# One of four column blocks of each MLP's second product made by seven half-block products (Strassen)

## The chip, the cores and the metric

The kernel runs on one core of a Trainium2 chip. The metric is the device time of one execution in microseconds (us). Three timed runs of the kernel before took 2242.58, 2242.69 and 2243.5 us; their median is 2242.69 us. The trace shown here is of one further, profiled execution of 2241.86 us, whose first and last instructions are 2240.1 us apart (its span). The engines are TensorE (PE; its weight loads are shown as PEld), VectorE (DVE), ScalarE (ACT), GpSimd (POOL) and SyncE (SP, whose queue issues the loads of weights).

## What is computed

A two-layer transformer over 256 tokens of width 2048 in float32. Layer 0 has stick-breaking attention, layer 1 a sparse attention of three branches; each is followed by an MLP with squared ReLU, 2048 to 8192 to 2048. The part that matters:

```python
def rms_norm(x, g):
    y = xf * lax.rsqrt(jnp.mean(xf * xf, axis=-1, keepdims=True) + NORM_EPS)
    return (y * g).astype(x.dtype)

def sqrelu_mlp(h, w1, w2):
    return jnp.square(jax.nn.relu(h @ w1)) @ w2

for layer in range(2):
    h = h + attention[layer](rms_norm(h, norm_g[layer]), ...)
    h = h + sqrelu_mlp(rms_norm(h, mlp_norm_g[layer]), mlp_w1[layer], mlp_w2[layer])
```

## The kernel before

**Products in three parts.** Every float32 product is made of three products of rounded parts: a matrix is split into `hi`, its value rounded to the matrix engine's float32r form, and `lo`, the rest; `x@w` is made as xhi·whi + xlo·whi + xhi·wlo, all gathered in one PSUM bank. `split` (line 122) makes `hi` on ScalarE (line 124) and `lo` on VectorE (line 126) for each chunk of weights, 128 partitions by 2 times 512 values, 512 KB, which `load` (line 131) brings through SP's queue. There are five buffers for raw chunks, four for `hi` and four for `lo`. A load waits until an older chunk's `lo` is made; a `hi` waits until TensorE has done with an older `hi`.

**The MLP** (`mlp`, line 351) goes through the 8192 hidden values in four groups `fg` of 2048. In a group's first product, four blocks `fb` of 512 hidden values are made transposed by `proj_T2` (line 185): eight chunks a block, each eight matmuls over 512 columns (line 192) and eight over 256 (line 198), into four PSUM banks. Lines 363 to 372 turn each pair of banks into squared ReLU values: ScalarE copies half a bank (`part`, line 367), VectorE adds the other half (`pre`, line 368) and forms max(a, 0)·a (`sq`, line 370), ScalarE rounds it (`yhi`, line 371) and VectorE makes the rest (`ylo`, line 372). The norm's factor is not in y: its square `r2` (line 361), one number per token, is multiplied in where a result is added to `h`.

In the group's second product, y is multiplied with four column blocks `nb` of w2, one after the other. Each is eight calls of `chunk_N` (line 142), a chunk being two rows of 128 hidden values by 512 columns; twelve matmuls over 512 columns (line 146), eight with `hi` and then four with `lo`, into two banks, one per half of the tokens. `add_h` (line 314) adds the two banks, times r2, to `h`.

**PSUM** has eight banks in two pools of four, `acc` and `att`. The blocks `fb` take acc and att in turn; the second product takes acc for nb 0 and 1 and att for nb 2 and 3 (acc for all in a layer's last group).

**The order of the work.** A scheduler lays out each engine's instructions when the program is built; on the chip every engine goes through its own list strictly in that order. Generators that are spawned (`spawn`, `pump`, lines 101 to 114) put pieces of other work between the chunks: `next_x` (line 287) transposes the new h into the next product's input, one block after `done(nb)`. `bcast_rows` (line 307) lays a per-token factor out along a row, by two small TensorE transposes (line 311).

Of the kernel before, what the change touches and what calls it, by code (L numbers as in the profile page):

```python
# [8 lines left out]
F32 = mybir.dt.float32  # L9
F32R = mybir.dt.float32r  # L10
AF = mybir.ActivationFunctionType
OP = mybir.AluOpType
# [3 lines left out]
P = 128  # L16
T = 256
NT = T // P
D = 2048
KD = D // P  # L20
# [19 lines left out]
def hybrid_kernel(  # L40
# [9 lines left out]
    wraw = ctx.enter_context(tc.tile_pool(name="wraw", bufs=5))  # L50
    whi = ctx.enter_context(tc.tile_pool(name="whi", bufs=4))
    wlo = ctx.enter_context(tc.tile_pool(name="wlo", bufs=4))
    acc = ctx.enter_context(tc.tile_pool(name="acc", bufs=4, space=PSUM))
    att = ctx.enter_context(tc.tile_pool(name="att", bufs=4, space=PSUM))

# [45 lines left out]
    def spawn(gen, rate, wait=0.0, first=False):  # L101
        beside.insert(0 if first else len(beside), [gen, rate, -wait])
# [122 lines left out]
    def evac_T2(dst, ps, row):  # L225
# [4 lines left out]
            nc.vector.tensor_tensor(dst[:, j, :], ps[j][:, :T], c[:, j, :], op=OP.add)  # L230
        nc.vector.tensor_tensor(dst, dst, row.unsqueeze(1).to_broadcast([P, 2, T]), op=OP.mult)

    def proj_N(src, n0, pool=acc, tag="acc"):
# [88 lines left out]
    def add_out(nb, ps, scale, ov):  # L322

        for t in range(NT):
            for i in range(2):
                w = NB // 2
                c = slice(nb * NB + i * w, nb * NB + (i + 1) * w)
                nc.vector.scalar_tensor_tensor(
                    h[:, t, c], ps[t][:, i * w:(i + 1) * w], scale[:, t:t + 1], h[:, t, c], op0=OP.mult, op1=OP.add
                )  # L330
                (nc.sync, nc.scalar)[i].dma_start(ov[:, t, c], h[:, t, c])

    def out_proj(src, layer, g0):
# [16 lines left out]

    def mlp(l, layer, junk, done, last=None):
        w1, w2 = mlp_w1[l], mlp_w2[l]
        r2 = None
        for fg in range(DFF // D):
            for fb in range(D // NB):
                ps = [bank(*((acc, "acc"), (att, "att"))[fb % 2]) for _ in range(NB // P)]
                proj_T2(ps, w1, fg * D + fb * NB)
                if r2 is None:
                    rstd = make_rstd(layer)
                    r2 = small.tile([P, NT], F32, tag="r2", name="r2")  # L360
                    nc.vector.tensor_tensor(r2, rstd, rstd, op=OP.mult)
# [11 lines left out]
            for nb in range(D // NB):  # L373
                end = last is not None and fg == DFF // D - 1 and nb == D // NB - 1
                pool = (att, "att") if nb >= 2 and fg < DFF // D - 1 else (acc, "acc")
                ps = [bank(*pool) for _ in range(NT)]
                for k0 in range(0, KD, KC):
                    chunk_N(ps, w2, fg * KD + k0, nb * NB, k0 == 0, k0 + (KC, 2 * KC)[end] == KD, yhi, ylo, koff=fg * KD,
                            by_token=end and k0 + KC == KD)
                if end:  # L380
                    add_out(nb, ps, r2, last)
                    return
                add_h(nb, ps, r2)
                if fg == DFF // D - 1:
                    done(nb)


    with tc.tile_pool(name="sbp", bufs=2) as sp:
# [195 lines left out]
    nc.vector.tensor_copy(peT, ppe[:, :2 * CL])  # L584

    with tc.tile_pool(name="m0p", bufs=2) as mp:
        def done0(nb):
            spawn(next_x("nsa", nb, G_NSA), 1)

        mlp(0, "m0", mp, done0)  # L590

# [350 lines left out]
        out_proj(nsa_w_out[0], "m1", G_M1)  # L942

    with tc.tile_pool(name="m1p", bufs=2) as mp:
        ov = out[0].rearrange("(t p) d -> p t d", p=P)
# [35 lines left out]
```

## Time and profile before

| | |
|---|---|
| median of three runs | 2242.69 us |
| profiled execution | 2241.86 us |
| its span | 2240.1 us |
| TensorE matmuls busy | 2231.1 us, 100% |
| TensorE weight loads busy | 1876.6 us, 84% |
| VectorE busy | 1309.9 us, 58% |
| ScalarE busy | 1099.1 us, 49% |
| granted TensorE clock, mean | 1.00 (2.4 GHz) |
| DMA | 405.86 MB, 181 GB/s |

Busy is the time in which at least one instruction of the engine was under way; neighbouring matmuls overlap, so the mean length of one matmul is longer than the step from one to the next. The chain of waits gives the steps: a piece of it is so many matmuls in so much time. In the same way a line of the timeline gives when an instruction began, and the difference of two beginnings is what one instruction really holds its engine for when the next stands ready.

The trace has the first MLP from 403 to 1123 us and the second from 1518 us to the end; in each, a group's first product takes about 90 us and its second about 89 us.

### The profile page before, as it was taken

What the parts mean: (1) busy time and instruction counts of PE and PEld (TensorE: products, weight loads), DVE (VectorE), ACT (ScalarE), POOL (GpSimd) and SP (SyncE); (2) the same over time, 40 slices, a digit from 0 to 9 for tenths busy, and PEclk for the clock granted to TensorE, in tenths of its full rate; (3) what the DMA queues carried; (4) which work ended last, traced back from release to release, by engine and by line L of the source; (5) the groups of instructions that cost most, each with busy time, mean ns of one, the idle gap of its engine ahead of it and who ended that gap; (6) DMA issues with size and microseconds to landing.
All of it is one profiled execution on the core that took longest, in us unless ns stands there. A gap on an engine that the chain in (4) does not pass through costs nothing.

```text
span 2240.1 us, 29460 instructions
## 1 busy us (share of the span) xinstructions
PE 2231.1 (100%) x11342; PEld 1876.6 (84%) x11342; DVE 1309.9 (58%) x1706; ACT 1099.1 (49%) x1591; POOL 43.1 (2%) x75
## 2 busy tenths in 40 slices
PE   9999999999999999999999999999999999999999
PEld 9888888888888888888887888888888888888887
DVE  5656655564555465556577877755655555654554
ACT  5555665443444344345455666655434434443442
POOL 0000000000000000000000011000000000000000
PEclk9999999999999999999999999999999999999999
DMA  6655555665665665665567554456656656656664
GB/s 228 201 166 170 166 166 181 185 187 188 189 188 188 189 188 188 189 188 188 179 177 218 160 142 142 133 167 184 188 185 192 188 187 190 186 185 193 187 197 136
DMA packets 260758, 405.86 MB, mean 181 GB/s; under 512 B 13189, under 2 KB 91913, under 8 KB 260617
## 3 DMA queue, kind: packets, MB, share of 16 engines
q1 hardware_dynamic: 259800, 403.52, 58.9%
q8 instruction: 89, 1.46, 0.3%
q10 hardware_dynamic: 816, 0.46, 0.1%
q14 instruction: 53, 0.43, 0.1%
HBM read 401.83 MB, written 2.10 MB: 180 GB/s over the span
## 4 chain that ended last, share of the span: by engine, by line
PE 99%; DVE 0%; POOL 0%; ACT 0%; issue 0%; DVEq 0%; ACTq 0%; POOLq 0%
PE acc L146 39%; PE att L146 13%; PE acc L192 11%; PE att L192 11%; PE att L198 5%; PE acc L198 5%; PE acc L212 5%; PE acc L218 3%; PE acc L175 2%; PE att L262 1%; PE att L814 1%; PE att L806 0%; PE att L807 0%; PE att L808 0%; PE att L502 0%; PE att L550 0%
## 5 line engine op out<-in xcount | busy, mean ns | idle before, releaser
L126 DVE TENSOR_TENSOR lo<-raw,hi 128x1024 fp32r<-128x1024 f32 x751 | 918.0, 1224 | 757.7 <-ACT hi L124 747.3
L124 ACT ACTIVATE hi<-raw 128x1024 fp32r<-128x1024 f32 x751 | 795.2, 1060 | 1032.1 <-PE acc L146 374.9
L146 PE MATMUL acc<-hi,yhi 128*128 128x512 f32 x892 | 354.0, 397 | 0.0
L146 PE MATMUL acc<-hi,ylo 128*128 128x512 f32 x892 | 351.6, 394 | 0.0
L192 PE MATMUL acc<-xs,hi 128*128 128x512 f32 x1024 | 259.6, 395 | 0.0
L192 PE MATMUL att<-xs,hi 128*128 128x512 f32 x1024 | 259.1, 395 | 0.0
L146 PE MATMUL acc<-lo,yhi 128*128 128x512 f32 x892 | 244.5, 395 | 0.0
L192 PEld LDWEIGHTS acc<-xs,hi 128*128 128x128 f32 x1024 | 184.0, 188 | 34.7 <-DVE h L318 0.3
L192 PEld LDWEIGHTS att<-xs,hi 128*128 128x128 f32 x1024 | 183.7, 188 | 33.9
L146 PEld LDWEIGHTS acc<-hi,yhi 128*128 128x128 f32 x892 | 168.1, 188 | 38.1 <-ACT yhi L248 0.2
L146 PEld LDWEIGHTS acc<-lo,yhi 128*128 128x128 f32 x892 | 167.4, 188 | 38.8 <-issue 0.4
L146 PEld LDWEIGHTS acc<-hi,ylo 128*128 128x128 f32 x892 | 168.1, 188 | 37.6 <-DVE ylo L249 0.2
L146 PE MATMUL acc<-hi,xs 128*128 128x512 f32 x704 | 180.0, 396 | 0.0
L146 PEld LDWEIGHTS acc<-hi,xs 128*128 128x128 f32 x704 | 130.7, 188 | 28.7
L146 PE MATMUL att<-hi,ylo 128*128 128x512 f32 x384 | 151.6, 395 | 0.0
L146 PE MATMUL att<-hi,yhi 128*128 128x512 f32 x384 | 151.5, 394 | 0.0
L198 PEld LDWEIGHTS att<-xs,lo 128*128 128x128 f32 x1024 | 139.3, 188 | 11.8
L198 PEld LDWEIGHTS acc<-xs,lo 128*128 128x128 f32 x1024 | 139.3, 188 | 11.8
L198 PE MATMUL att<-xs,lo 128*128 128x256 f32 x1024 | 142.2, 281 | 0.0
L198 PE MATMUL acc<-xs,lo 128*128 128x256 f32 x1024 | 142.2, 281 | 0.0
L212 PE MATMUL acc<-xs,hi 128*128 128x512 f32 x512 | 130.5, 396 | 0.0
L212 PEld LDWEIGHTS acc<-xs,hi 128*128 128x128 f32 x512 | 91.9, 188 | 17.5 <-DVE xs L269 0.3
(234 smaller groups left out, 1942.4 us busy)
## 6 DMA issues: line engine op xcount, KB each, us to landing
raw<-in_mlp_w_dram SPq DMA_DIRECT2D x512, 512.0 KB, 3.9
raw<-in_sb_w_qkv_dram SPq DMA_DIRECT2D x95, 512.0 KB, 3.8
raw<-in_nsa_w_in_dram SPq DMA_DIRECT2D x50, 512.0 KB, 3.6
raw<-in_sb_w_out_dram SPq DMA_DIRECT2D x32, 512.0 KB, 3.8
raw<-in_nsa_w_in_dram SPq DMA_DIRECT2D x64, 256.0 KB, 3.2
raw<-in_nsa_w_out_dram SPq DMA_DIRECT2D x32, 512.0 KB, 3.9
w1t<-in_nsa_cmp_w_dram SPq DMA_DIRECT2D x8, 512.0 KB, 4.0
h<-in_x_dram SPq DMA_DIRECT2D x8, 256.0 KB, 4.3
```

The source lines that it names most:

```text
L124: nc.scalar.activation(hi, raw, AF.Copy)
L126: nc.vector.tensor_tensor(lo, raw, hi.bitcast(F32), op=OP.subtract)
L146: mm = lambda a, b, k, t, s, e: nc.tensor.matmul(ps[t], a[:, k, t * P:(t + 1) * P], b, start=s, stop=e)
L175: nc.tensor.matmul(o, w[:, kk, m * P:(m + 1) * P], x[:, k0 + kk, :], start=s, stop=e, skip_group_check=True)
L192: nc.tensor.matmul(ps[m], hi[:, kk, m * P:(m + 1) * P], xs[:, k0 + kk, :, :].rearrange("p a t -> p (a t)"), start=k0 + kk == 0, stop=k0 + ...
L198: nc.tensor.matmul(ps[m][:, :T], lo[:, kk, m * P:(m + 1) * P], xhi[:, k0 + kk, :], start=False, stop=k0 + kk == KD - 1, skip_group_check=True,
L212: nc.tensor.matmul(ps[m], hi[:, kk, m * P:(m + 1) * P], xs[:, k0 + kk, :, :].rearrange("p a t -> p (a t)"), start=k0 + kk == 0, stop=k0 + ...
L218: nc.tensor.matmul(ps[m][:, :T], lo[:, kk, m * P:(m + 1) * P], xhi[:, k0 + kk, :], start=False, stop=k0 + kk == KD - 1, skip_group_check=True,
L262: nc.tensor.transpose(ps[:, j * T + t * P:j * T + (t + 1) * P], h[:, t, (kp + j) * P:(kp + j + 1) * P], ident)
L814: nc.tensor.transpose(ptp[:w, j * P:(j + 1) * P], src(j), ident)
```

## The change

In each group of both MLPs, the column block nb = 2 is no longer made by twelve matmuls over 512 columns a chunk but by Strassen's scheme (Winograd's form) on the 2-by-2 blocks that a chunk and the two halves of the tokens form: seven products, each half a block wide. With three rounded parts each, that is 21 matmuls over 256 columns a chunk (`chunk_S`), into seven half banks. For this:

- sums of y blocks (`sums`, split into the tile `ss`) are made where y is made, 128 columns each, four per pair of banks;
- sums of the weights' blocks (`ts`) are made on VectorE for each chunk of block 2, and then split like a chunk, so that such a chunk takes two of the four `hi` buffers and two of the four `lo` buffers;
- the seven half banks are put together and added to `h` by `add_S`;
- the norm's factor goes into y, as (max(a, 0)·r)², since the sums run over tokens: `row` holds r along the tokens (by `bcast_rows`, once in each MLP), line 370 becomes a multiplication with it, and the square is made on ScalarE. `add_h` and `add_out` lose their factor;
- the order of the second product changes. Chunks of block 2 stand between chunks of blocks 0 and 1, one after every two; block 3 follows alone. In a layer's last group the order begins with two chunks of block 2, and `done` is called for blocks 0 to 2 together when block 3 begins. The two PSUM pools change their roles from group to group, since block 2 now holds four banks.

```diff
+    def chunk_S(ps, src, k0, n0, first, last, ahi, alo, shi, slo, koff=0):
+        W = NB // 2
+        raw = load(src, k0, KC, n0, NB)
+        flat = raw.rearrange("p k n -> p (k n)")
+        ts = wsum.tile([P, 4, W], F32, tag="ts", name="ts")
+        b12 = flat[:, 3 * W:].unsqueeze(1).to_broadcast([P, 2, W])
+        nc.vector.tensor_tensor(ts[:, :2, :], flat[:, W:3 * W].rearrange("p (a n) -> p a n", a=2), b12, op=OP.subtract)
...
+        nc.scalar.activation(hi[:, :3 * W], flat[:, :3 * W], AF.Copy)
+        nc.vector.tensor_tensor(ts[:, 2, :], ts[:, 0, :], flat[:, 2 * W:3 * W], op=OP.add)
+        nc.vector.tensor_tensor(ts[:, 3, :], flat[:, :W], ts[:, 2, :], op=OP.subtract)
+        thi, tlo = split(ts)
+        nc.vector.tensor_tensor(lo[:, :3 * W], flat[:, :3 * W], hi[:, :3 * W].bitcast(F32), op=OP.subtract)
...
+        for i, xh, xl, wh, wl in trivial + sums:
+            mm(i, xh, wh, first and i in (0, 1, 6, 4), False)
+            mm(i, xl, wh, False, False)
+        pump()
+        for i, xh, xl, wh, wl in sums + trivial:
+            mm(i, xh, wl, False, last)
+        pump()
...
+    def add_S(nb, bs, ps, pool):
...
+        nc.scalar.activation(u[:, 0, :], ps[0], AF.Copy)
+        nc.vector.tensor_tensor(v[:, 0, :], ps[5], u[:, 0, :], op=OP.add)
+        nc.vector.tensor_tensor(u[:, 1, :], ps[4], v[:, 0, :], op=OP.add)
+        nc.vector.tensor_tensor(v[:, 1, :], ps[6], v[:, 0, :], op=OP.add)
+        nc.vector.tensor_tensor(hb[0], bs[1], hb[0], op=OP.add)
+        nc.vector.tensor_tensor(hb[1], bs[2], hb[1], op=OP.add)
+        nc.vector.tensor_tensor(hb[0], hb[0], u.rearrange("p a n -> p (a n)"), op=OP.add)
+        hv = hb[1].rearrange("p (a n) -> p a n", a=2)
+        nc.vector.tensor_tensor(hv, hv, v[:, 1, :].unsqueeze(1).to_broadcast([P, 2, W]), op=OP.add)
...
+        def rows():
+            yield
+            pb = bcast_rows(make_rstd(layer))
+            nc.scalar.activation(row, pb[:, :T], AF.Copy)
...
                         nc.vector.tensor_tensor(a[:, j, :], ps[2 * b + j][:, :T], c[:, j, :], op=OP.add)
+                    nc.vector.scalar_tensor_tensor(
+                        a, a, 0.0, row.unsqueeze(1).to_broadcast([P, 2, T]), op0=OP.max, op1=OP.mult
+                    )
                     s = junk.tile([P, 2, T], F32, tag="sq", name="sq")
-                    nc.vector.scalar_tensor_tensor(s, a, 0.0, a, op0=OP.max, op1=OP.mult)
+                    nc.scalar.activation(s, a, AF.Square)
                     nc.scalar.activation(yhi[:, k:k + 2, :], s, AF.Copy)
                     nc.vector.tensor_tensor(ylo[:, k:k + 2, :], s, yhi[:, k:k + 2, :].bitcast(F32), op=OP.subtract)
+                    a1, a2 = [[s[:, kk, t * P:(t + 1) * P] for kk in (1, 0)] for t in range(NT)]
+                    q = junk.tile([P, 4, P], F32, tag="sums", name="sums")
+                    nc.vector.scalar_tensor_tensor(q[:, 0, :], a2[0], -1.0, a2[1], op0=OP.mult, op1=OP.subtract)
+                    nc.vector.tensor_tensor(q[:, 2, :], a1[0], a2[0], op=OP.subtract)
+                    nc.vector.tensor_tensor(q[:, 1, :], a2[1], q[:, 2, :], op=OP.subtract)
+                    nc.vector.tensor_tensor(q[:, 3, :], a1[1], q[:, 1, :], op=OP.subtract)
+                    split_evac(ss[:, 0, k // 2], ss[:, 1, k // 2], q)
...
+            for i in range(NK):
+                pq = [(j // NK, j % NK) for j in (2 * i, 2 * i + 1)]
+                order += [(2, i)] + pq if end else pq + [(2, i)]
+            if end:
+                order.insert(1, order.pop(3))
+            order += [(3, i) for i in range(NK)]
...
+            group1(fg, ((A, B), (B, A))[fg % 2])
+            group2(fg, *((A, B) if end or fg % 2 == 0 else (B, A)), end)
...
-            spawn(next_x("nsa", nb, G_NSA), 1)
+            spawn(next_x("nsa", nb, G_NSA), 1.5)
```

What this makes of the engines' lists is seen at two places. The first is TensorE, at the first chunk of block 2 in the first MLP's first group (line 147 of the new kernel is line 146 of the old one; line 268 is `chunk_S`; `ss` holds the sums of y).

```order
L147 MATMUL acc<-lo,yhi 128x512 x4
L268 MATMUL att<-hi,yhi 128x256
L268 MATMUL att<-hi,ylo 128x256
L268 MATMUL att<-hi,yhi 128x256
L268 MATMUL att<-hi,ylo 128x256
L268 MATMUL att<-hi,ss 128x256 x8
L268 MATMUL att<-hi,yhi 128x256
L268 MATMUL att<-hi,ylo 128x256
L268 MATMUL att<-lo,ss 128x256 x3
L268 MATMUL att<-lo,yhi 128x256 x3
L268 MATMUL att<-lo,ss 128x256
```

Between two plain chunks there now stand 14 matmuls with a `hi` (six with the chunk's own, eight with that of its sums) and 7 with a `lo`, all over 256 columns and into the att pool.

The second is VectorE where the first MLP's last group goes over from its first to its second product. Before, the list there is this (lines 368 to 372 are the last block's way from PSUM to y, line 126 is the `lo` of chunks to come):

```order
L126 TENSOR_TENSOR lo<-raw,hi 128x1024 x6
L368 TENSOR_TENSOR pre<-att,part 128x256 x3
L370 SCALAR_TENSOR_TENSOR sq<-pre 128x512
L368 TENSOR_TENSOR pre<-att,part 128x256
L126 TENSOR_TENSOR lo<-raw,hi 128x1024
L372 TENSOR_TENSOR ylo<-sq,yhi 128x512
L370 SCALAR_TENSOR_TENSOR sq<-pre 128x512
L126 TENSOR_TENSOR lo<-raw,hi 128x1024
```

In the changed kernel the same place reads as follows (line 127 is the old line 126, the first row of it for the sums of the second chunk of block 2; line 250 the `lo` of that chunk itself; lines 439, 440 and 446 the old 368, 370 and 372; lines 450 to 453 the sums of y):

```order
L127 TENSOR_TENSOR lo<-ts,hi 128x1024
L439 TENSOR_TENSOR pre<-acc,part 128x256 x3
L440 SCALAR_TENSOR_TENSOR pre<-pre,row 128x512
L439 TENSOR_TENSOR pre<-acc,part 128x256
L250 TENSOR_TENSOR lo<-raw,hi 128x768
L450 SCALAR_TENSOR_TENSOR sums<-sq 128x128
L446 TENSOR_TENSOR ylo<-sq,yhi 128x512
L451 TENSOR_TENSOR sums<-sq 128x128
L440 SCALAR_TENSOR_TENSOR pre<-pre,row 128x512
L452 TENSOR_TENSOR sums<-sq,sums 128x128
L127 TENSOR_TENSOR lo<-raw,hi 128x1024
```

The last row is the `lo` of the first plain chunk, the third chunk that TensorE takes in this product. Five instructions stand before it that follow on ScalarE's square of the same block.

## Rows read from the trace of the kernel before

**Rows 1.** The page: busy time of each engine with its share of the span, and two of its rows of tenths in 40 slices.

```profile
PE 2231.1 (100%) x11342; PEld 1876.6 (84%) x11342; DVE 1309.9 (58%) x1706; ACT 1099.1 (49%) x1591; POOL 43.1 (2%) x75
...
PE   9999999999999999999999999999999999999999
...
DVE  5656655564555465556577877755655555654554
```

**Rows 2.** The chain of waits in order of time: start in us, length in us, engine, pool and line, number of matmuls. The first pieces are of a stretch of the first product and the turn to the second (first MLP, group 0); the next lie in the first projection, where matmuls over 256 columns alone follow each other.

```profile
485.65 1.86 PE att L192 x8
487.51 0.94 PE att L198 x8
...
494.08 44.61 PE acc L146 x192
...
43.49 5.70 PE acc L175 x48
...
49.62 8.54 PE acc L175 x72
...
1031.47 27.89 PE acc L146 x120
```

**Rows 3.** Groups of the page and of the list by line: line, engine, operation, tiles, shapes, number | busy us, mean ns of one | idle us before. The short matmul and its weight load.

```profile
L198 PEld LDWEIGHTS acc<-xs,lo 128*128 128x128 f32 x1024 | 139.3, 188 | 11.8
...
L198 PE MATMUL acc<-xs,lo 128*128 128x256 f32 x1024 | 142.2, 281 | 0.0
```

**Rows 4.** Busy time by stretch (us): length, then busy time and number of instructions of PE, PEld, DVE, ACT and POOL, the granted clock, the DMA engines' busy share and GB/s. The first stretch is a first product, the second a second product.

```profile
403.00:494.00 91.00, 91.00 (x522) 79.56 (x522) 53.07 (x66) 43.50 (x59) 0.70 (x1) 1.00 0.62 185
494.00:583.00 89.00, 89.00 (x385) 72.18 (x384) 46.80 (x46) 35.97 (x39) 0.00 (x0) 1.00 0.60 189
```

**Rows 5.** Groups of VectorE and then of ScalarE with shapes kept apart, columns as in rows 3.

```profile
L126 DVE TENSOR_TENSOR lo<-raw,hi 128x1024 fp32r<-128x1024 f32 x751 | 918.0, 1224 | 757.7 <-ACT hi L124 747.3 <-PE acc L146 2.8 <-ACT e L510 2.6
L372 DVE TENSOR_TENSOR ylo<-sq,yhi 128x512 fp32r<-128x512 f32 x64 | 43.7, 683 | 0.0
L370 DVE SCALAR_TENSOR_TENSOR sq<-pre 128x512 f32<-128x512 f32 x64 | 43.7, 682 | 0.0
...
L320 DVE SCALAR_TENSOR_TENSOR h<-acc,r,h 128x512 f32<-128x512 f32 x38 | 26.8, 746 | 22.2 <-PE acc L146 22.2
...
L368 DVE TENSOR_TENSOR pre<-acc,part 128x256 f32<-128x256 f32 x64 | 23.9, 415 | 0.0
...
L318 DVE TENSOR_TENSOR h<-acc,h 128x512 f32<-128x512 f32 x16 | 10.3, 686 | 7.7 <-PE acc L146 7.6
...
L615 DVE TENSOR_SCALAR dist<-dg 128x128 f32<-128x128 f32 x2 | 0.5, 278 | 0.0
...
L124 ACT ACTIVATE hi<-raw 128x1024 fp32r<-128x1024 f32 x751 | 795.2, 1060 | 1032.1 <-PE acc L146 374.9 <-PE acc L192 186.9 <-PE att L146 179.3
L371 ACT ACTIVATE yhi<-sq 128x512 fp32r<-128x512 f32 x64 | 40.1, 627 | 2.9 <-DVE sq L370 0.5
...
L367 ACT ACTIVATE part<-acc 128x256 f32<-128x256 f32 x64 | 19.0, 381 | 0.0
```

**Rows 6.** The timeline of VectorE and then of ScalarE where the first MLP's last group turns to its second product (at 1031.47 us, rows 2): start, length in us, engine, line, operation, tiles, shapes, number, and in brackets the idle time before and what ended it.

```profile
1031.66 1.23 DVE L126 TENSOR_TENSOR lo<-raw,hi 128x1024 fp32r<-128x1024 f32 x1 [1.58 <-ACT hi L124]
1032.80 1.08 DVE L368 TENSOR_TENSOR pre<-att,part 128x256 f32<-128x256 f32 x3
1033.80 0.68 DVE L370 SCALAR_TENSOR_TENSOR sq<-pre 128x512 f32<-128x512 f32 x1
1034.40 0.42 DVE L368 TENSOR_TENSOR pre<-att,part 128x256 f32<-128x256 f32 x1
1034.73 1.21 DVE L126 TENSOR_TENSOR lo<-raw,hi 128x1024 fp32r<-128x1024 f32 x1
1035.86 0.68 DVE L372 TENSOR_TENSOR ylo<-sq,yhi 128x512 fp32r<-128x512 f32 x1
1036.47 0.68 DVE L370 SCALAR_TENSOR_TENSOR sq<-pre 128x512 f32<-128x512 f32 x1
1037.29 1.22 DVE L126 TENSOR_TENSOR lo<-raw,hi 128x1024 fp32r<-128x1024 f32 x1
...
1030.57 1.06 ACT L124 ACTIVATE hi<-raw 128x1024 fp32r<-128x1024 f32 x1 [1.75 <-PE att L192]
1031.53 1.18 ACT L367 ACTIVATE part<-att 128x256 f32<-128x256 f32 x4
1033.37 1.06 ACT L124 ACTIVATE hi<-raw 128x1024 fp32r<-128x1024 f32 x1 [0.66 <-PE acc L146]
```

**Rows 7.** The list of waits (who waited for whom: us in total, times, longest us), and of the page the loads of the MLPs' weights (number, KB each, median us from issue to landing).

```profile
DVE lo L126 <- ACT hi L124: 747.3, 553, 2.2
...
ACT hi L124 <- PE acc L146: 374.9, 244, 2.6
...
raw<-in_mlp_w_dram SPq DMA_DIRECT2D x512, 512.0 KB, 3.9
```

**Rows 8.** The chain of waits near the start of layer 1, columns as in rows 2: the two transposes of `bcast_rows`.

```profile
1133.63 0.22 PE att L311 x2
```

More of the change, by code (lines that the diff above doesn't have):

```diff
@@ L231, in evac_T2, with mm @@
         nc.vector.tensor_tensor(dst, dst, row.unsqueeze(1).to_broadcast([P, 2, T]), op=OP.mult)
+    def chunk_S(ps, src, k0, n0, first, last, ahi, alo, shi, slo, koff=0):
[5 more added lines that the diff above has]
+        nc.vector.tensor_tensor(ts[:, :2, :], flat[:, W:3 * W].rearrange("p (a n) -> p a n", a=2), b12, op=OP.subtract)
+        hi = whi.tile([P, KC, NB], F32R, tag="hi", name="hi").rearrange("p k n -> p (k n)")
+        lo = wlo.tile([P, KC, NB], F32R, tag="lo", name="lo").rearrange("p k n -> p (k n)")
+        nc.scalar.activation(hi[:, :3 * W], flat[:, :3 * W], AF.Copy)
[3 more added lines that the diff above has]
+        nc.vector.tensor_tensor(lo[:, :3 * W], flat[:, :3 * W], hi[:, :3 * W].bitcast(F32), op=OP.subtract)
+        k = k0 - koff
+        y = lambda a, kk, t: a[:, k + kk, t * P:(t + 1) * P]
+        s = lambda a, i: a[:, k // KC, i, :]
+        b = lambda w, i: w[:, i * W:(i + 1) * W]
+        trivial = [
+            (0, y(ahi, 1, 0), y(alo, 1, 0), b(hi, 2), b(lo, 2)),
+            (1, y(ahi, 0, 0), y(alo, 0, 0), b(hi, 0), b(lo, 0)),
+            (2, s(shi, 3), s(slo, 3), b(hi, 1), b(lo, 1)),
+        ]
+        sums = [
+            (6, s(shi, 2), s(slo, 2), thi[:, 0, :], tlo[:, 0, :]),
+            (4, s(shi, 0), s(slo, 0), thi[:, 1, :], tlo[:, 1, :]),
+            (5, s(shi, 1), s(slo, 1), thi[:, 2, :], tlo[:, 2, :]),
+            (3, y(ahi, 0, 1), y(alo, 0, 1), thi[:, 3, :], tlo[:, 3, :]),
+        ]
+        def mm(i, a, w, s, e):
+            nc.tensor.matmul(ps[i], a, w, start=s, stop=e, skip_group_check=True)
+        for i, xh, xl, wh, wl in trivial + sums:
[5 more added lines that the diff above has]
+        pump()
@@ new lines, in banks_S @@
+    def banks_S(pool, tag):
+        W = NB // 2
+        bs = [bank(pool, tag) for _ in range(4)]
+        half = lambda j, i: bs[j][:, i * W:(i + 1) * W]
+        return bs, [half(0, 0), half(1, 0), half(1, 1), half(2, 0), half(2, 1), half(3, 1), half(3, 0)]
+    def add_S(nb, bs, ps, pool):
+        W = NB // 2
+        u = pool.tile([P, 2, W], F32, tag="part", name="u")
+        v = pool.tile([P, 2, W], F32, tag="pre", name="v")
+        hb = [h[:, t, nb * NB:(nb + 1) * NB] for t in range(NT)]
+        nc.scalar.activation(u[:, 0, :], ps[0], AF.Copy)
[7 more added lines that the diff above has]
+        nc.vector.tensor_tensor(hv, hv, v[:, 1, :].unsqueeze(1).to_broadcast([P, 2, W]), op=OP.add)
@@ L327, in add_out @@
                 c = slice(nb * NB + i * w, nb * NB + (i + 1) * w)
-                nc.vector.scalar_tensor_tensor(
-                    h[:, t, c], ps[t][:, i * w:(i + 1) * w], scale[:, t:t + 1], h[:, t, c], op0=OP.mult, op1=OP.add
-                )
+                nc.vector.tensor_tensor(h[:, t, c], ps[t][:, i * w:(i + 1) * w], h[:, t, c], op=OP.add)
                 (nc.sync, nc.scalar)[i].dma_start(ov[:, t, c], h[:, t, c])
@@ L352, in mlp, with group1 @@
         w1, w2 = mlp_w1[l], mlp_w2[l]
-        r2 = None
-        for fg in range(DFF // D):
+        ss = junk.tile([P, 2, KD // 2, 4, P], F32R, name="ss", bufs=1)
+        row = junk.tile([P, T], F32, name="row", bufs=1)
+        def rows():
+            yield
+            pb = bcast_rows(make_rstd(layer))
+            nc.scalar.activation(row, pb[:, :T], AF.Copy)
+        def group1(fg, pools):
             for fb in range(D // NB):
-                ps = [bank(*((acc, "acc"), (att, "att"))[fb % 2]) for _ in range(NB // P)]
+                ps = [bank(*pools[fb % 2]) for _ in range(NB // P)]
                 proj_T2(ps, w1, fg * D + fb * NB)
[L358 to L361, printed above, removed]
                 for b in range(2):
@@ L371, in mlp @@
                     nc.scalar.activation(yhi[:, k:k + 2, :], s, AF.Copy)
                     nc.vector.tensor_tensor(ylo[:, k:k + 2, :], s, yhi[:, k:k + 2, :].bitcast(F32), op=OP.subtract)
[L373 to L385, printed above, removed]
+                    a1, a2 = [[s[:, kk, t * P:(t + 1) * P] for kk in (1, 0)] for t in range(NT)]
@@ new lines, in group2 @@
+        def group2(fg, plain, strassen, end):
+            NK = KD // KC
+            order = []
+            for i in range(NK):
[4 more added lines that the diff above has]
+            order += [(3, i) for i in range(NK)]
+            for nb, i in order:
+                k0 = fg * KD + i * KC
+                args = (w2, k0, nb * NB, i == 0, i == NK - 1, yhi, ylo)
+                if nb == 2:
+                    if i == 0:
+                        bs, s = banks_S(*strassen)
+                    chunk_S(s, *args, ss[:, 0], ss[:, 1], koff=fg * KD)
+                    if i == NK - 1:
+                        add_S(nb, bs, s, junk)
+                    continue
+                if i == 0:
+                    ps = [bank(*plain) for _ in range(NT)]
+                    if end and nb == 3:
+                        for n in range(3):
+                            done(n)
+                out = last is not None and end and nb == 3
+                chunk_N(ps, w2, k0, nb * NB, i == 0, i == NK - (2 if out else 1), yhi, ylo, koff=fg * KD,
+                        by_token=out and i == NK - 1)
+                if i == NK - 1:
+                    if out:
+                        add_out(nb, ps, last)
+                        return
+                    add_h(nb, ps)
+                    if end and nb == 3:
+                        done(nb)
@@ L388, in hybrid_kernel @@
+        spawn(rows(), 1)
+        A, B = (acc, "acc"), (att, "att")
+        for fg in range(DFF // D):
+            end = fg == DFF // D - 1
+            group1(fg, ((A, B), (B, A))[fg % 2])
+            group2(fg, *((A, B) if end or fg % 2 == 0 else (B, A)), end)
     with tc.tile_pool(name="sbp", bufs=2) as sp:
@@ L944, in hybrid_kernel @@
     with tc.tile_pool(name="m1p", bufs=2) as mp:
+        wsum = mp
         ov = out[0].rearrange("(t p) d -> p t d", p=P)
```

4 lines of the change are left out of this document (3 added, 1 removed).

## The prediction

> **What bounds the kernel now.** I read the page first. TensorE is busy for 2231.1 us of a span of 2240.1, in every one of 40 slices, while VectorE has 58% and ScalarE 49% [rows 1]. So one asks first how many TensorE steps there are, and only then whether another engine comes late. The chain of waits confirms it: it runs from one TensorE piece to the next without a gap, and it gives the steps [rows 2]. In the second product 192 matmuls over 512 columns take 44.61 us: 232.3 ns each, 2.788 us for a chunk of twelve. Where matmuls over 256 columns alone follow each other, 72 take 8.54 us: 118.6 ns each; the 48 before them give 118.8. Eight between longer ones take 0.94 us, 117.5 ns each. The short step is thus 0.51 of the long one, although a weight load is listed with 188 ns [rows 3]: the loads lie over the matmuls and over each other.
>
> The list of waits says how VectorE and ScalarE stand. `lo` waits for `hi` 747 us in total, and `hi` waits for TensorE to give back a buffer [rows 7]; both run as far ahead as four buffers allow, and idle. By stretch, VectorE works 53 us of 91 in a first product and 47 of 89 in a second [rows 4]. There is room, but the change spends it: that is where to look for a loss.
>
> **What the change takes away.** A chunk of block 2 has 21 short matmuls in place of twelve long ones: 21 × 118.7 ns = 2.493 us for 2.788, so 0.295 us less. There are 8 chunks × 4 groups × 2 MLPs = 64: 18.9 us less. The bounds of this term come from the rows: at 117.5 ns the chunk takes 2.468 us and the gain is 20.5 us; from the other side, the short matmul's group is listed as busy 142.2 us for 1024, 139 ns each [rows 3], which would make the chunk 2.92 us, 0.13 longer than now, a loss of 8.4 us. I take 118.7, since only the chain's pieces measure a step, and the longest of them hold nothing but short matmuls that alternate between banks as these do.
>
> **What it adds on TensorE.** Two small transposes per MLP for `row`; such a pair took 0.22 us [rows 8]: 0.44 us. They wait for the factor that GpSimd makes, but stand after the fifth chunk of the first block, about 14 us into it (5 × (1.86 + 0.94), rows 2); I add no wait.
>
> **What it adds on VectorE and ScalarE.** For a chunk of block 2, VectorE makes the weight sums (512, 256 and 256 columns) and two `lo` (1024 and 768) instead of one of 1024. With mean durations [rows 5] of 0.68 and 0.415, with 1.22, and with 0.95 for 768, which lies between 512 and 1024, that is 3.69 us. The chunk alone would so be VectorE's, but two plain chunks stand beside each: TensorE needs 2 × 2.788 + 2.493 = 8.07 us for the three, VectorE 2 × 1.22 + 3.69 = 6.14, ScalarE 2 × 1.06 + 0.84 + 1.06 = 4.02. Covered, with 1.9 us to spare; without the cover 64 chunks would lose 1.2 us each.
>
> For each pair of banks in the first product VectorE gets four operations of 128 columns (0.28 each, rows 5 have one of that size) and a rest of 0.68, ScalarE a square and a rounding of 0.63 each. A block of 22.5 us has two pairs: 3.6 us more for VectorE, 2.5 for ScalarE. VectorE comes to 53 + 4 × 3.6 = 67 of 91 us. Hidden by `lo` standing over three chunks ahead: in the rows it is started 0.2 us into the second product for the fourth chunk of it [rows 6]. `add_S` is 4.0 us (three of 0.415, four of 0.68) where `add_h` took 1.5; the list puts it behind the `lo` of two later chunks, and eight plain chunks follow, so it is hidden.
>
> DMA: the same 512 KB a chunk, in 8.07 us for three instead of 8.36; the engines are at 0.60 [rows 4], a load lands after 3.9 us [rows 7] and is issued some ten before it is wanted. Nothing.
>
> **Where it comes late.** Now the turn from the first to the second product, where the last block's way to y and the double work of a chunk of block 2 meet on VectorE. In six of the eight groups a chunk of block 2 comes third. Counting from the turn with the mean durations, VectorE frees the last PSUM bank that this chunk writes at 3.8 us (wanted at 5.6), has its `lo` at 4.8 (wanted 7.7), the third plain chunk's at 8.3 (wanted 9.9), the second block-2 chunk's at 14.4 (wanted 15.8). Nothing waits, with 0.8 us to spare at the tightest, the third chunk of block 2.
>
> In each MLP's last group two chunks of block 2 come first, so that four buffers hold both and the first plain chunk's `hi` must wait for them. TensorE reaches the plain chunk at 4.98 us and its `lo` at 4.98 + 8 × 0.232 = 6.84. On VectorE, the `lo` of the second chunk's sums can begin at 0.2, as the one in rows 6 does, since the buffer is the same. What then holds the engine is the step from beginning to beginning [rows 6]: 1.13 for 1024 columns, 0.61 for 512, 0.33 for 256, and about 0.87 for 768 and 0.2 for 128. The `lo` and four `pre` with the multiplication between them end at 3.3, the 768 at 4.1; then the list has a sum that follows on the square. ScalarE is past the four `part` at 1.24 and makes the two plain `hi` (1.06 each) first, then square and rounding (0.63 each): 4.6. So `ylo` runs until 5.25, the next sum, multiplication and sum until 6.25, and only then comes the plain chunk's `lo`, done at 7.5: TensorE waits 0.7 us. For the next plain chunk the same reckoning gives 0.14 us. Per MLP 0.85 us; with the mean durations instead of the steps it would be 1.9, and zero if ScalarE makes the square before the second `hi`. I take 0.85, as the rows of the same place show the steps: 1.7 us for both, at most 4.
>
> **The sum.** It is made against the profiled execution: 2241.86 − 18.9 + 0.44 + 1.7 = 2225.1 us. The median of the runs shown is 0.83 us above that execution; the forecast is 2225.1 + 0.83 = 2226 us, 0.74% less.
>
> **Rival 1: a short matmul costs a fixed part, and the change is slower.** Each product adds nine matmuls a chunk, 576 in all, each with its own weight load of 188 ns, taken from three tiles in turn. The place is TensorE in `chunk_S`. The point from which it decides is 2.788/21 = 132.8 ns a short matmul: above it the chunk is longer than now. At the 139 ns of rows 3 the time is 2241.86 + 8.4 + 2.1 + 0.83 = 2253 us. For it speaks that this pattern of weights has not run yet, and that loads are busy 84% of the time; against it speak the 72 short matmuls in a row, each with its load, at 118.6 [rows 2]. From the two steps, a fixed part of only 5 ns follows (2 × 118.7 − 232.3). The Trainium skill, on the page "TensorE: Matmul & The Clock Gate", section "Back-to-back issue gap", gives 81 ns a matmul at 128 columns and 131 at 512 for a stream of loads and matmuls, so a large fixed part: estimated from that page, 98 ns at 256, 2.05 us for 21 and 1.57 for twelve, and the change would lose 31 us. The trace's 232.3 at 512 does not agree with it. I give this rival 6 in 100.
>
> **Rival 2: VectorE is late at every turn.** If the six other turns lose what the last one would by mean durations, 1.9 us each, because VectorE stands before a `ts` whose raw chunk has not landed, and what follows in its list stands with it, the loss is 11.4 us more: 2237 us. For it speaks that six `ts` are put ahead of older `lo` in the list and that the margins are 0.8 to 1.8 us; against it that loads are issued over three chunks ahead and the mean durations, with which I counted, are longer than the steps. 15 in 100. It would need 18.9/8 = 2.3 us at every turn to eat the whole gain.
>
> **Rival 3: no wait at all.** ScalarE and VectorE are some tenths faster at the last turn, and the short step is 117.5 ns: 2242.69 − 20.5 + 0.4 = 2222.6 us. It lies beside the forecast; both together have 75 in 100 (2222 to 2231). The last 4 are for something not seen here.
>
> **How the numbers follow.** What a measurement can tell from no change is about 0.2%, 4.5 us. Forecast, rival 2 and rival 3 are all faster than 2238.2 but for the far end of rival 2: 0.89 faster, 0.03 the same, and 0.08 slower, which is rival 1 with part of the unseen. The range has to hold 8 in 10: from 2220 (under rival 3 by its uncertainty) to 2237, rival 2's middle.
>
> **What would show it.** In the profile after: `chunk_S`'s 7 and 14 matmuls at steps of 117 to 120 ns in the chain, a TensorE total lower by some 18 us, and VectorE near 72% of the span. Waits of TensorE on the `lo` of the first plain chunk in each MLP's last group, about 0.7 us, and none at the other six turns. A step above 125 ns would show rival 1 at work; waits of TensorE on `lo` or PSUM at 20 us after each turn rival 2. I am wrong if VectorE's list holds TensorE in the steady part, where I count 1.9 us of room.

## The result and the profile after

The changed kernel took 2226.74 us (median of four runs, 2223.00 to 2230.95) beside 2242.93 us for the kernel before; the ratio is 0.9928, with an interval of 0.9905 to 0.9951. The forecast was 2226 us. No run lies near the median: two took 2223.0 and 2223.6 us, two 2229.9 and 2231.0, and the trace is of one of the faster pair. The number came out, but its working did not: two things that the prediction left out, each some 20 us, nearly cancel. The profile gives them away where its parts do not fit together. The page of the profiled execution (2223.57 us):

```profile
span 2221.8 us, 31529 instructions
...
PE 2197.6 (99%) x11922; PEld 1880.5 (85%) x11922; DVE 1542.2 (69%) x2320; ACT 1226.2 (55%) x1793; POOL 43.4 (2%) x75
```

Against [rows 1], TensorE's busy time fell by 33.5 us, where some 18 were forecast, and the span by only 18.3: TensorE now works less than was reckoned and waits for the rest. The list of TensorE's waits (who waited for whom: us in total, times, longest), and from the page the group of the weight sums `ts` (columns as in rows 3), say for what:

```profile
PE att L268 <- DVE lo L127: 7.5, 8, 1.5
PE acc L268 <- DVE lo L127: 4.7, 4, 1.6
...
PE acc L147 <- DVE lo L127: 1.1, 2, 0.5
```

```profile
L243 DVE TENSOR_TENSOR ts<-raw 128x512 f32<-128x512 f32 x64 | 44.2, 691 | 103.8 <-DMA raw<-in_mlp_w_dram 103.8
```

The first two rows of the list are waits in `chunk_S`, nearly all of them in the steady part, where none was forecast; only the third is the forecast wait at the last groups' turn. VectorE stood 103.8 us in front of `ts`, waiting for a load.

**The loop.** The chain of waits in the first MLP's group 1, and VectorE's timeline of the same stretch (columns as in rows 2 and 6; line 127 is the old 126, `split`; 250 is the `lo` of 768 columns):

```profile
705.85 1.23 DVE lo L127
...
707.09 5.40 DMA raw<-in_mlp_w_dram
...
712.51 0.03 DVE ts L243
...
713.12 1.22 DVE lo L127
714.34 0.88 DVE lo L250
...
715.27 0.64 PE acc L268 x3
...
715.92 1.23 DVE lo L127
...
717.17 4.93 DMA raw<-in_mlp_w_dram
```

```profile
705.85 2.36 DVE L127 TENSOR_TENSOR lo<-raw,hi 128x1024 fp32r<-128x1024 f32 x2
712.51 0.69 DVE L243 TENSOR_TENSOR ts<-raw 128x512 f32<-128x512 f32 x1 [4.31 <-DMA raw<-in_mlp_w_dram]
713.12 1.22 DVE L127 TENSOR_TENSOR lo<-ts,hi 128x1024 fp32r<-128x1024 f32 x1
714.26 0.95 DVE L250 TENSOR_TENSOR lo<-raw,hi 128x768 fp32r<-128x768 f32 x1
715.13 0.42 DVE L247 TENSOR_TENSOR ts<-ts,raw 128x256 f32<-128x256 f32 x1
715.58 0.42 DVE L248 TENSOR_TENSOR ts<-raw,ts 128x256 f32<-128x256 f32 x1
715.92 2.35 DVE L127 TENSOR_TENSOR lo<-raw,hi 128x1024 fp32r<-128x1024 f32 x2
722.13 0.69 DVE L243 TENSOR_TENSOR ts<-raw 128x512 f32<-128x512 f32 x1 [3.85 <-DMA raw<-in_mlp_w_dram]
```

Read it as a ring. A plain chunk's `lo` ends at 707.08 and frees a raw buffer; the load for the next chunk of block 2 starts at 707.09 and lands at 712.49. VectorE's next but one instruction is the `ts` that needs this load. So it stands for 4.31 us, and only then makes two older `lo`, for which TensorE waits already. The `lo` that frees the next buffer stands behind them. (In the chain it follows three matmuls of TensorE, which end just as VectorE comes free.) The ring takes 9.62 us from `ts` to `ts` (722.13 − 712.51); TensorE needs 8.0 for the same three chunks.

The two `ts` shown are those of the seventh and eighth chunk of block 2. In the six groups that are not an MLP's last, these two stand for 3.85 to 4.5 us each, 12 of the 64 `ts` in all; the earlier ones stand for 0 to 2.9 us, some of them with more work between them and the `lo` that frees their buffer (at the sixth chunk of this group it stands six places ahead, and the wait is 1.56 us). TensorE waits accordingly late: 48 and 57 us after the turn, at the sixth and seventh chunk of block 2, in each MLP's first group at the seventh alone. One of these waits, 1.5 us at 2008 us, is followed by a granted clock of 0.50 (the 1.2 GHz level) from 2010 to 2013 us; the others are not.

**The shorter steps.** In parts of the kernel that the change does not touch, TensorE's steps are shorter than in [rows 2]. The chain, first in the first projection and then at the turn of the first MLP's group 0:

```profile
44.18 5.46 PE acc L176 x48
...
50.08 8.18 PE acc L176 x72
...
486.94 1.86 PE att L193 x8
488.80 0.91 PE att L199 x8
489.71 5.49 PE acc L147 x24
495.20 2.46 PE att L268 x21
497.66 5.50 PE acc L147 x24
503.17 2.50 PE att L268 x21
```

The 48 matmuls of the projection took 5.70 us before and take 5.46 now (118.8 and 113.8 ns each), a plain chunk's step fell from 232.3 to 229 ns. `chunk_S`'s 21 take 2.46 or 2.50 us, 117 to 119 ns, as forecast.

What the diff does to the first projection is nothing but this: `r2` is gone from the pool `small`, two buffers of 32 bytes, and everything laid out behind it, `raw`, `hi` and `lo`, lies 64 bytes earlier in SBUF in the whole program (by the addresses of the built programs, the first `hi` at byte 128960 of each partition for 129024). `xs`, `yhi` and `ylo` stay (32896, 65664 and 82048).

### The profile page after: what moved, and what is told of

The parts are those of the page before. It is cut to its first block, busy times and chain, and to the rows that moved or that the text cites. A ratio compares the mean times of both kernels' runs of the same rounds, so it can differ in the third digit from the quotient of the medians.

```text
span 2221.8 us, 31529 instructions
## 1 busy us (share of the span) xinstructions
PE 2197.6 (99%) x11922; PEld 1880.5 (85%) x11922; DVE 1542.2 (69%) x2320; ACT 1226.2 (55%) x1793; POOL 43.4 (2%) x75
## 4 chain that ended last, share of the span: by engine, by line
PE 91%; DMA 4%; DVE 4%; issue 1%; ACT 0%; POOL 0%; DVEq 0%; ACTq 0%; SPq 0%; POOLq 0%
PE acc L147 33%; PE acc L193 11%; PE att L193 11%; PE att L147 6%; PE acc L213 5%; PE att L199 5%; PE acc L199 5%; DMA raw<-in_mlp_w_dram 4%; PE att L268 4%; PE acc L219 3%; DVE lo L127 2%; PE acc L176 2%; PE acc L268 1%; DVE lo L250 1%; PE att L331 1%
## 5 line engine op out<-in xcount | busy, mean ns | idle before, releaser
L125 ACT ACTIVATE hi<-raw 128x1024 fp32r<-128x1024 f32 x687 | 726.5, 1060 | 717.9 <-PE acc L147 268.0
L127 DVE TENSOR_TENSOR lo<-raw,hi 128x1024 fp32r<-128x1024 f32 x687 | 834.7, 1223 | 401.1 <-ACT hi L125 379.8
L147 PE MATMUL acc<-hi,yhi 128*128 128x512 f32 x828 | 327.0, 395 | 0.0
L147 PE MATMUL acc<-hi,ylo 128*128 128x512 f32 x828 | 325.0, 393 | 0.0
L147 PE MATMUL acc<-lo,yhi 128*128 128x512 f32 x828 | 225.3, 393 | 1.1 <-DVE lo L127 1.1
L147 PEld LDWEIGHTS acc<-lo,yhi 128*128 128x128 f32 x828 | 154.8, 188 | 35.6 <-DVE lo L127 1.9
L147 PEld LDWEIGHTS acc<-hi,yhi 128*128 128x128 f32 x828 | 155.9, 188 | 31.7 <-ACT yhi L317 0.2
L147 PEld LDWEIGHTS acc<-hi,ylo 128*128 128x128 f32 x828 | 156.0, 188 | 31.3 <-DVE ylo L318 0.2
L199 PEld LDWEIGHTS acc<-xs,lo 128*128 128x128 f32 x1024 | 135.9, 188 | 11.6
L199 PEld LDWEIGHTS att<-xs,lo 128*128 128x128 f32 x1024 | 135.9, 188 | 11.6
L243 DVE TENSOR_TENSOR ts<-raw 128x512 f32<-128x512 f32 x64 | 44.2, 691 | 103.8 <-DMA raw<-in_mlp_w_dram 103.8
L125 ACT ACTIVATE hi<-ts 128x1024 fp32r<-128x1024 f32 x64 | 67.6, 1056 | 65.1 <-DVE ts L248 46.7
```

What stands on the lines that cost most here:

```text
L125: nc.scalar.activation(hi, raw, AF.Copy)
L127: nc.vector.tensor_tensor(lo, raw, hi.bitcast(F32), op=OP.subtract)
L199: nc.tensor.matmul(ps[m][:, :T], lo[:, kk, m * P:(m + 1) * P], xhi[:, k0 + kk, :], start=False, stop=k0 + kk == KD - 1, skip_group_check=True,
L243: nc.vector.tensor_tensor(ts[:, :2, :], flat[:, W:3 * W].rearrange("p (a n) -> p a n", a=2), b12, op=OP.subtract)
```

## The experiments

The theories: A, where `raw`, `hi` and `lo` lie sets TensorE's step, and the gain is that of the shift; B, its rival, the seven products gave the gain themselves. C, the shared raw buffers hold VectorE in the ring; D, its rival, VectorE is late for another reason, such as its added work. Each time is a median, and each ratio is to the kernel before, timed beside it.

**e1: the kernel before with the shift alone.** Only the tile's pool is changed:

```diff
-                    r2 = small.tile([P, NT], F32, tag="r2", name="r2")
+                    r2 = junk.tile([P, NT], F32, name="r2", bufs=1)
```

> The kernel before, with only its tile r2 moved from the pool `small` to the MLP's own pool; all of hi, lo and raw then begin 64 bytes earlier in SBUF, as in the changed kernel. Theory A (the 64 bytes make TensorE's steps shorter): steps of 229 ns over 512 columns and 114 over 256 in place of 232.3 and 118.6, no new waits, and a time of 2226 to 2231 us. Rival B (the changed kernel's profiled execution merely ran on faster steps, whatever its addresses): steps and time as before, 2242 to 2244 us.

2215.02 us (2213.85 to 2217.55), ratio 0.9877 [0.9862, 0.9891]. Moving one tile of two numbers gives 27 us, more than A expected, and more than the whole change. From the chain, the first projection and the first MLP's second product:

```profile
42.51 5.47 PE acc L175 x48
...
487.82 43.95 PE acc L146 x192
```

192 matmuls in 43.95 us for 44.61 [rows 2]: 228.9 ns for 232.3.

**e2: the changed kernel without the shift**, by an unused tile in the place of `r2`:

```diff
+    pad = small.tile([P, NT], F32, tag="r2", name="r2")
+    nc.gpsimd.memset(pad, 0.0)
```

> The changed kernel with 64 bytes of `small` kept by an unused tile, so that hi, lo and raw lie where they lay in the kernel before. Theory A: steps of 232 and 118.6 ns again, and 2232 to 2240 us, since the seven products alone are worth 18.9 us less the waits. Rival B: 2223 to 2231 us as the changed kernel, with its shorter steps.

2244.30 us (2238.80 to 2247.35), ratio 1.0005 [0.9996, 1.0014]. At the old addresses the change is worth nothing, less even than A expected. A holds, B falls.

**e3: raw buffers of its own for the chunks of block 2**, at the new addresses, and **e4**, the same at the old ones (with e2's pad):

```diff
-        raw = load(src, k0, KC, n0, NB)
+        raw = wsum.tile([P, KC, NB], F32, tag="rs", name="rs")
+        nc.sync.dma_start(raw, src[k0 * P:(k0 + KC) * P, n0:n0 + NB].rearrange("(k p) n -> p k n", p=P))
```

> The changed kernel with two raw buffers of their own for the chunks of block 2, beside the five that the other chunks use. Theory C (TensorE waits because VectorE stands before `ts`, whose load is issued only when the `lo` two places before it in VectorE's list gives back its raw buffer): TensorE's waits on `lo` fall from 13.3 us to under 3, VectorE's idle time before `ts` for a load from 104 us to under 15, and the time is 2210 to 2216 us. Rival D (VectorE simply has too much to do beside these chunks, or the loads land late because the DMA engines are busy): waits of 8 us or more remain, on `lo` and not on loads, and the time is above 2219 us.

> Both edits: raw buffers of their own for block 2's chunks, and 64 bytes kept so that hi, lo and raw lie as in the kernel before. Theories A and C together: 2223 to 2228 us, which is the kernel before less the 18.9 us of the seven products, the two transposes and about 2 us of waits. Rival B: as the third run, 2210 to 2216 us.

e3: 2210.64 us (2208.42 to 2211.73), ratio 0.9853 [0.9836, 0.9869]. e4: 2232.73 us (2232.05 to 2234.30), ratio 0.9955 [0.9940, 0.9970], 5 us above what A and C together expected. The buffers gain 16.1 us at the new addresses and 11.6 at the old ones (differences to the changed kernel and to e2). In e3 VectorE's idle time before `ts` falls from 103.8 to 17.6 us, and the six groups that are not an MLP's last take 85.84 us each, where the changed kernel has 87.9 to 90.9 (table below). C holds for the ring, since VectorE's work is the same. That the sharing is at fault and not the number of buffers is not shown: e3 also has two buffers more, and seven shared ones have no run. And the waits did not all go: under 15 us was expected where 17.6 are left, and under 3 us of TensorE's waits on `lo` where 5.8 are left. The list of waits of e3:

```profile
DVE ts L244 <- DMA rs<-in_mlp_w_dram: 17.6, 16, 4.0
...
PE acc L147 <- DVE lo L127: 4.3, 2, 2.2
...
PE att L269 <- DVE lo L127: 0.9, 2, 0.5
...
PE att L269 <- DVE lo L251: 0.6, 2, 0.3
```

The two waits of 2.2 us are the turns of the two last groups. The chain there (e3, first MLP; lines 440 to 454 are y's way) and busy time by stretch (columns as in rows 4):

```profile
1009.10 0.88 DVE lo L251
...
1010.04 3.83 DMA rs<-in_mlp_w_dram
...
1013.96 0.69 DVE ts L244
1014.65 0.99 DVE pre L440 x3
...
1022.24 1.15 DVE lo L127
1023.38 0.04 issue
1023.43 8.61 PE acc L147 x24
```

```profile
1020.00:1030.00 10.00, 7.53 (x21) 5.65 (x20) 9.82 (x17) 4.50 (x7) 0.00 (x0) 0.66 0.61 193
1030.00:1040.00 10.00, 10.00 (x55) 8.63 (x55) 6.00 (x6) 4.24 (x5) 0.00 (x0) 1.00 0.62 207
```

It is the ring's mechanism once more. Two chunks of block 2 in front use up the two own buffers; the third one's `ts` is early in VectorE's list, stands 4.00 us on its load, and the last block's y and the first plain chunk's `lo` are queued behind it. The wait has a second price: over the 10 us that hold it the granted clock is 0.66 (from 1023 to 1029 us it is 0.50, the 1.2 GHz level), and 24 plain matmuls take 8.61 us instead of 5.50. The price is not paid each time: in e4's second MLP a wait of 2.2 us at the same place is followed by a granted clock of 1.00.

**e5: the last groups laid out as the others**, on top of e3:

```diff
-                order += [(2, i)] + pq if end else pq + [(2, i)]
-            if end:
-                order.insert(1, order.pop(3))
+                order += pq + [(2, i)]
...
-            group2(fg, *((A, B) if end or fg % 2 == 0 else (B, A)), end)
+            group2(fg, *((A, B) if fg % 2 == 0 else (B, A)), end)
```

> The changed kernel with raw buffers of its own for the chunks of block 2 (as e3), and with the last group of each MLP laid out as the other groups: two plain chunks, then one of block 2, and the two PSUM pools in the same alternation. In e3 the six other groups take 85.84 us each, the last ones 95.1 and 91.0, and in the chain of these the second weight sum of a block-2 chunk stands 4 us on its load while the last block's y is queued behind it. Theory E (the order with two block-2 chunks in front is what costs): the last groups come to 85.8 and 88.5 us (the first MLP's holds 2.7 us of transposes), no wait of TensorE on lo over 0.5 us, 2198 to 2203 us. Rival F (the last group is dear for what follows it, h, the transposes, the three calls of done at once, whatever the order): 2206 to 2213 us, with waits of TensorE on h or on a PSUM bank in the place of those on lo.

2199.65 us (2198.13 to 2201.25), ratio 0.9808 [0.9791, 0.9824]. No wait on a `lo` is left; the last groups take 88.56 and 85.75 us. E holds.

**e6 to e8: what about the address counts?** All three are the kernel before. In e6 `r2` is moved as in e1, and 64 bytes are put in front of `h`; in e7 `r2` is moved and 64 bytes are put between the pools `wraw` and `whi`; in e8 only the latter.

```diff
+    cpad = cpool.tile([P, 16], F32, name="cpad")
...
     h = cpool.tile([P, NT, D], F32, name="h")
...
+    gap = ctx.enter_context(tc.tile_pool(name="gap", bufs=1))
     whi = ctx.enter_context(tc.tile_pool(name="whi", bufs=4))
...
+    gp = gap.tile([P, 16], F32, name="gp")
```

> The kernel before, with raw, hi and lo at their old addresses and xs, yhi and ylo 64 bytes further on: the distance between the two operands of a matmul is that of e1, the addresses of hi and lo are those of before. Theory G (the distance between the two operands sets the step): steps of 229 and 114 ns, 2213 to 2218 us. Rival H (where hi and lo themselves lie sets it): 232 and 119 ns, 2241 to 2244 us.

> The kernel before with the raw buffers 64 bytes earlier and hi and lo at their old addresses. If the operands of the matmuls are what counts (theories G and H): as before, 2241 to 2244 us, 232 and 119 ns. If it is the place into which the loads are written and from which ScalarE and VectorE read: 2213 to 2218 us, 229 and 114 ns.

> The kernel before with hi and lo 64 bytes further on in place of 64 earlier, all else where it was. If only a place of hi and lo at a whole multiple of 2048 bytes is dear: 2213 to 2218 us as in e1. If the step changes with the distance to xs, yhi and ylo (now 64 bytes, before 128, in e1 192, each in the remainder by 2048): not 229 and 114 ns, but as before or longer, 2241 to 2270 us.

e6: 2214.75 us, ratio 0.9878 [0.9863, 0.9892], as e1. e7: 2242.77 us, ratio 1.0001 [0.9991, 1.0010]. So it is neither the place of `hi` and `lo` alone nor the raw buffers, but the distance between a matmul's two operands (G). e8: 2230.90 us, ratio 0.9949 [0.9934, 0.9964]: below the 2241 that the second theory expected, and not 2215 either. Its chain shows why; the first product gains where the second loses:

```profile
489.72 1.83 PE att L195 x8
491.55 0.94 PE att L201 x8
492.49 44.80 PE acc L149 x192
```

In the first product `xs` moves and `hi` is the weights' side; in the second it is the other way round, so one shift changes the two distances in opposite senses. The layouts tried make one table, by the distance of the moving operand from the stationary one in the remainder by 256 (step in ns from the chain's pieces, or, marked *, the mean of the beginnings in the trace):

| distance | 512 columns | 256 columns |
|---|---|---|
| 0 (`hi` with `ss`) | | 119.6* |
| 64 | 228.9 (e1, `hi` with y), 228.8 (e8, `xs` with `hi`) | 117.8 (e8, first projection, 72 in 8.48 us), 115.7* (e8, `xs` with `lo`) |
| 128 (before) | 232.3 | 118.7 |
| 192 | 233.3 (e8, `hi` with y), 232.5 (e1, `xs` with `hi`) | 113.8 (e1, `xs` with `lo`) |

A mean can hide differences: in e8's second product all operands are 192 apart, and yet the matmuls of `hi` with `yhi` take 230.7 ns, of `lo` with `yhi` 233.5 and of `hi` with `ylo` 235.9 (means of the beginnings).

**e9 to e12: the table used, and the change at the old addresses.** e9 is e5 with 64 bytes in front of `ss`; e10 is e5 with e2's pad; e11 is e5 with `hi` laid by use; e12 is e9 and e11 in one, with two small tiles sharing a place.

```diff
+        pad = junk.tile([P, 16], F32, name="pad", bufs=1)
...
         ss = junk.tile([P, 2, KD // 2, 4, P], F32R, name="ss", bufs=1)
...
+    def split(raw, off=0):
...
+        hi = whi.tile([P, KC * NB + 64], F32R, tag="hi", name="hi")[:, off:off + n]
...
+            hi, lo = load_split(src, k0, KC, n0, NB, off=32)
```

> As e5, with the tile ss (the sums of y) 64 bytes further on, so that it no longer lies at a whole multiple of 256 bytes from hi and lo. In e5 the matmuls on ss have a step of 119.6 ns, while the 256-column matmuls of xs with lo, whose operands are 192 bytes apart in the remainder by 256, have 114. Theory G (the distance of the two operands sets the step, in the remainder by 256): 12 of 21 products of a chunk get 3 to 6 ns shorter, 2 to 4.5 us in all, 2195 to 2198 us. Rival (the short step of chunk_S comes from its changing banks and weights, whatever the distance): 119 to 120 ns, 2198 to 2201 us.

> As e5, with raw, hi and lo back at the addresses of the kernel before (two small unused tiles take the place of r2): what the seven products are worth by themselves when neither a load nor the last groups' order holds VectorE up. The prediction's own term is 18.9 us less and 0.44 more, without its 1.7 for the turn: all eight groups at 86.83 us (and 2.7 for the transposes of the first MLP's last), 2222 to 2226 us. If the short products lose elsewhere what they save: over 2230 us.

> As e5, with each hi tile 256 bytes longer, and hi laid 128 bytes further into it where it is the weights' side (the products that are made transposed), so that both kinds of product have their moving operand 64 bytes beyond the stationary one in the remainder by 256. e8 had that distance for the 512-column matmuls of xs: 228.9 ns where e1 has 232.3. Theory G: a chunk of the first product 8 x 3.4 = 27 ns shorter, 256 chunks in the MLPs, 7 us, and 1 to 2 us in the attention's products: 2190 to 2194 us, first products of 87.8 to 88.0 us in place of 88.75. Rival (the gain of e8 was that of lo or of something else that moved): 2198 to 2201 us.

> e9 and e11 together: own raw buffers, the last groups laid out as the others, ss 64 bytes further on, hi laid 128 bytes into its tile where it is the weights' side (two small tiles share a place so that all of it fits, which moves raw, hi and lo by 512 bytes, no part of the remainder by 256). If the two gains are of different matmuls, as theory G has it, they add: e5's 2199.65 less 7.6 (e9) less 7.3 (e11), 2183 to 2187 us; first products of 87.9 us, second of 85.0. If the distance counts in the remainder by 2048, the shift by 512 shows as steps of 232 and 119 ns again: over 2200 us.

e9: 2192.09 us, ratio 0.9778 [0.9760, 0.9795]; the chunks of block 2 take 2.38 us, 113.3 ns a matmul, a larger gain than expected: not only the matmuls on `ss` are shorter but those on y too, 113.3 ns for 115 to 118 in e5 (means of the beginnings), though their own two operands lie as they did. So the neighbours in the row count as well, and the table is not the whole rule. e10: 2223.86 us, ratio 0.9919 [0.9903, 0.9935]. e11: 2192.35 us, ratio 0.9777 [0.9762, 0.9793], first products of 87.91 us. e12: 2185.09 us (2184.81 to 2186.74), ratio 0.9744 [0.9728, 0.9760]: the two gains add, and 58 us are gone from the kernel before. Its four `hi` buffers lie 4352 bytes apart, at four different remainders by 2048 but one by 256, and its steps are those of e9 and e11; so in these runs it is the remainder by 256 that counts (by 128, the distances 64 and 192 would be one, and their steps differ). The chain of e10 and of e12, each in the first MLP's second product, group 0:

```profile
497.48 5.57 PE acc L149 x24
503.05 2.50 PE att L271 x21
```

```profile
495.01 5.49 PE acc L149 x24
500.50 2.38 PE att L271 x21
```

## Why the prediction came out, step by step

The lengths of the MLPs' stages, from the first matmul of a product to the first of the next (the last group of all up to the beginning of its last matmul), put the terms side by side (us; the second MLP's groups after a slash):

| | before | e2 (change, old addresses) | e10 (ring and turn mended) | after |
|---|---|---|---|---|
| first product, group 0 | 90.91 / 90.93 | 91.13 / 91.15 | 91.13 / 91.17 | 90.00 / 90.04 |
| first product, the others | 89.91 | 89.93 | 89.93 | 88.75 |
| second product, group 0 | 89.22 / 89.22 | 89.21 / 90.66 | 86.83 / 86.83 | 87.93 / 88.24 |
| group 1 | 89.22 / 89.22 | 88.89 / 91.10 | 86.83 / 86.83 | 89.08 / 89.97 |
| group 2 | 89.22 / 89.22 | 88.75 / 91.11 | 86.83 / 86.83 | 89.09 / 90.85 |
| last group | 91.95 / 89.16 | 91.73 / 88.45 | 89.48 / 86.76 | 90.19 / 87.78 |

- **The seven products, −18.9 us: right.** In e10 a group falls by 2.39 us, 0.299 for each of its eight chunks; forecast 0.295. The whole kernel gains 18.1 us (2242.00 to 2223.86), forecast without the turn 18.5. Rival 1 is out: the 21 matmuls of `chunk_S` take 2.50 us, 119 ns each, where it needed over 132.8.
- **The two transposes, +0.44: right**, 0.22 and 0.24 us in group 0's first product.
- **VectorE's and ScalarE's added work in the first product, nothing: right**, 89.91 to 89.93 us.
- **The loads, "Nothing": this step failed.** They were said to be issued "some ten before" they are wanted, and VectorE to have "1.9 us to spare". The one was taken from the kernel before, the other was a count of work; what decides is which instruction frees the buffer. At the last two chunks of block 2 in a group it is a `lo` two places ahead of the `ts` in VectorE's own list, so the load has no lead but the time of these places, and about 4 of its 5 us stand in VectorE's list. Against e10 it costs e2 20.4 us with the turn. This is rival 2's mechanism, VectorE standing before a `ts` whose raw chunk has not landed; but it was placed some 20 us after the turns (measured: 48 and 57), priced at 11.4 us and dismissed with loads "issued over three chunks ahead". That fits the kernel before, where no wait on a load of the MLPs' weights is listed, but not this one. The prediction itself named the sign of being wrong: "if VectorE's list holds TensorE in the steady part". It does.
- **The last groups' turn, 0.85 us an MLP: right for this kernel in place and near in size.** The list has two waits of the first plain chunk on its `lo`, 1.1 us together, forecast 1.7. It is not the cost of this order in general: where the ring is mended, the same turn costs 2.2 us of waiting and, in three of four cases in e3 and e4, the clock.
- **What no step had: the lay of the tiles.** The prediction took the steps of [rows 2] as fixed. The removal of `r2` changed them everywhere, by 17.6 us for the changed kernel (e2 to after).

The sum as it was: 2242.0 − 18.1 (e10) + 20.4 (ring and turn, e2) − 17.6 (shift) = 2226.7 us. Forecast: 2242.7 − 18.9 + 0.4 + 1.7 = 2226. The sizes hold for this order of the steps: with the shift first they are −27.0 (e1), −15.4 (e1 to e5) and +27.1 (e5 to after). The change of the algorithm is worth its 18 us only once the ring is mended; as it stands, what was measured is the gain of 64 bytes. The two errors cancelled by chance.

Open: what in the chip makes the distance count was not tried (that a matmul also feels its neighbours' weights, e9, would fit the weight loads that lie over the matmuls), and distances between the multiples of 64 have no run. The changed kernel's four runs spread over 8 us, as e2's ten do, where e5's four stay within 3.2 and e12's within 2; that the ring or the clock costs more in some executions could explain it, but there is one trace of each.

## What to carry to other kernels

Before counting a transfer as hidden, name the instruction that frees its buffer and look where it stands in the list of the engine that will wait for the load: if it is the same engine and a few places earlier, the transfer's whole length is in the loop, whatever room the engine has by its busy time. When a change adds or removes any tile, however small, compare the steps of code that it does not touch; if they moved, time the kernel before with the same lay before crediting the change. A time that agrees with the forecast shows nothing until its terms agree too: here TensorE's busy time and the span already disagreed.

## What the hardware showed

A matmul's step depended on the distance in SBUF between its moving and its stationary operand, in the remainder by 256 bytes: 228.8 to 233.3 ns with 512 columns and 113.3 to 119.6 with 256 (means of rows of matmuls; the neighbours count too, e9). With TensorE busy all the time that was worth 27 us of 2242 for 64 bytes (e1). Of the distances tried, 64 was best for rows of 512 columns; for 256, 192 and a mixture of 64 and 192 (e9). And a wait of 2.2 us of TensorE was followed by a granted clock of 0.50, the 1.2 GHz level, from 1023 to 1029 us (e3, first MLP), which cost more than the wait: 24 matmuls took 3.1 us longer. In e4's second MLP a wait of the same length left the clock at 1.00; what tells the two apart was not tried.
